# Four modulation blocks of a hybrid diffusion layer move from matmuls to dot products, and head norms and softmax rows to ScalarE

## The chip, the cores and the metric

The kernel runs on one core of one Trainium2 chip. The metric is device time in microseconds (us) of one execution: 1324.15 us is the median of three runs of the kernel before (1323.88 to 1324.64). A core has five engines that each work through a queue of their own in order: TensorE (PE in the profile, with PEld for its weight loads), VectorE (DVE), ScalarE (ACT), GpSimd (POOL) and SyncE (SP), which here only issues DMA transfers.

## What is computed

One layer of a transformer for 128 context tokens and 128 latent tokens, with width 2048. The parts that matter here:

```python
sh1, sc1, g1, sh2, sc2, g2 = silu(cond) @ w_ada + b_ada      # six modulation vectors per group
h  = rms_norm(x, norm1_w) * (1 + sc1) + sh1
qa, ka, va, qb, kb, vb, ga, gb = split(h @ w_in)             # q, k get an RMS norm per head of 128
# mixer A: window attention with a sink; mixer B: neighbourhood attention with a bias
m  = (sigmoid(ga) * (oa @ w_br_a) + sigmoid(gb) * (ob @ w_br_b)) @ w_out
x  = x + g1 * m
h2 = rms_norm(x, norm2_w) * (1 + sc2) + sh2
x  = x + g2 * (relu(h2 @ w_up) ** 2 @ w_down)
```

There are two conditions (one for the context, one for the latents), so each modulation vector exists twice. A modulation vector has 16 blocks of 128 columns. Shift and scale of one norm together are called its modulations here.

## The kernel before

All of the large products run in float32 accuracy: a weight tile of 128x1024 (a half-step, 512 KB, `raw`) is rounded by ScalarE into a high part `wH` (L101), VectorE subtracts to get the low part `wL` (L260), and TensorE adds three products, high by high, low by high, high by low. The kernel is one list of steps, `wsteps`, of 512 KB each: steps 0 to 71 are the first nine column units of `w_in` (q, k, v of both mixers), 72 to 135 the gates, then the branches, `w_out`, the up and down projections to step 455. A step holds 12 matmuls of 512 columns. Everything else is hung on a step number: `at(i, ...)` runs a piece after the matmuls of step i, and the number tables at the head of the file say which step that is. `LOOK` says how many steps ahead of TensorE the high and low parts are made, `RUN` how far ahead the transfers are put into SP's queue (`load_at`).

The nine first units are computed in chunks of the contraction (`CHUNKS` = 2, 2, 2, 4, 6 blocks of h), so that the first steps need only the first blocks of h: blocks 0 and 1 for steps 0 to 8, 2 and 3 from step 9, 4 and 5 from 18, 6 to 9 from 27, 10 to 15 from 45. Each block of h needs its block of the modulations.

A block of the modulations is made in one of two ways.

- As matmuls (`pair_load`, `pair_mm_q`, L322 and L330): four transfers of 512 KB (`araw`, shift and scale together), then 16 float32 matmuls of 256 columns, four side by side in 32-column strips of the array; the trace has 32 records for them. Two blocks share a bank, so the trace shows them as groups of 64. ScalarE copies the bank out (`ada_evac`), one step later TensorE turns it by four transposes (`ada_cols`, L348) and VectorE sums it up. `ADA_AT` has the steps for norm 1, `SS_AT` for norm 2.
- As dot products (`dot_load`, `dot`, L1398 and L1411): per block, for each of shift and scale, two transfers of 512 KB (`aT`, halves of the contraction), and for each of these two VectorE instructions of 128x1024 (one for each condition), after which a short instruction reads the accumulator. They need the conditions spread over all partitions (`cB`, L1392, two transfers of 512 KB for a half of the contraction). `DOTS1` has the steps for norm 1; `DOTS` those for the gate of the first sub-layer and norm 2 together; `DOTS2` those for the last gate.

Before, 14 blocks of norm 1 (`FB1`) and 6 of norm 2 (`FB_DVE`) are matmuls, 2 and 10 dot products; both gates are dot products altogether.

Weights' low parts can also be made without VectorE: for the steps in `LO_DMA`, ScalarE writes minus the high part (L266) and GpSimd issues a transfer that reads the weights again and adds them to it (L267).

In steps 67 to 98 the head norms run (`qk_stat`, `qk_apply`, `qk_T`, with their steps in `POST`): ScalarE squares a group's 512 columns in one instruction (L671), VectorE sums by head (L673), GpSimd takes the root, then the context half is scaled by ScalarE head by head (L683), the latent half by VectorE in one instruction (L684), and TensorE transposes. Steps 79 to 123 hold eight attention jobs (`JOBS`): scores, softmax with `exp` and sums on ScalarE, `normalise` on VectorE (L795), transposes of the probabilities (L802) which ScalarE copies out (`probT`), and the products with the values (`ps_o`, L809 and L813).

## Time and profile before

| | |
|---|---|
| median of three runs | 1324.15 us |
| the profiled execution | 1324.28 us |
| its span, first to last instruction | 1322.5 us |
| TensorE busy | 1309.0 us (99%) |
| VectorE busy | 1151.4 us (87%) |
| ScalarE busy | 890.8 us (67%) |
| moved by DMA | 419.03 MB, 317 GB/s on average |

The profiled execution lasted 1.8 us longer than its span, and 0.13 us more than the median. Busy time of an engine counts overlapping instructions once. A matmul's record lasts about 390 ns while the next one starts 227 ns later, so a stretch of TensorE is read from one start to a later one and not from the means. The same holds for VectorE and ScalarE, whose records overlap the next by some 80 to 100 ns.

### The profile page before, as it was taken

How to read it: one execution, taken by the hardware profiler on the slowest of the kernel's cores; microseconds unless marked ns; L12 is line 12 of the kernel's file. 1: busy time of each engine (PE TensorE's matmuls, PEld its weight loads, DVE VectorE, ACT ScalarE, POOL GpSimd, SP SyncE). 2: the span in 40 equal slices, each digit the busy share in tenths (PEclk: the TensorE clock that was granted, in tenths of full speed). 3: DMA queues.
4: the chain of work that ended last, by engine and by line, in shares of the span. 5: the costliest groups of instructions: out<-in, count | busy, mean ns of one | idle time of the engine just before them, and what ended most of it. 6: DMA issues, size and time to landing. Idle time of an engine off the chain costs nothing.

```text
span 1322.5 us, 18220 instructions
## 1 busy us (share of the span) xinstructions
PE 1309.0 (99%) x6388; PEld 1061.3 (80%) x6388; DVE 1151.4 (87%) x1487; ACT 890.8 (67%) x1129; POOL 87.1 (7%) x109
## 2 busy tenths in 40 slices
PE   8999999999999999999999999999999999999998
PEld 4777788788888878888888888888888888888876
DVE  4578699988898999999789889898898998979996
ACT  5634656576565545755788877968879688796772
POOL 0000000512000000000100010100101001010011
PEclk9999999999999999999999999999999999999999
DMA  9999998887689999998489998888998799899996
GB/s 375 408 408 409 406 398 344 326 286 281 200 296 343 373 377 349 323 374 306 137 289 291 290 312 273 283 300 289 292 321 281 282 341 288 295 269 366 375 334 185
DMA packets 155260, 419.03 MB, mean 317 GB/s; under 512 B 52720, under 2 KB 53984, under 8 KB 155168
## 3 DMA queue, kind: packets, MB, share of 16 engines
q1 hardware_dynamic: 146128, 386.54, 80.1%
q0 software_dynamic: 8848, 31.23, 10.3%
q8 instruction: 50, 0.82, 0.2%
q14 instruction: 42, 0.34, 0.1%
q10 hardware_dynamic: 192, 0.10, 0.0%
HBM read 390.24 MB, written 17.61 MB: 308 GB/s over the span
## 4 chain that ended last, share of the span: by engine, by line
PE 93%; DMA 3%; DVE 2%; issue 1%; POOL 0%; ACT 0%; POOLq 0%; DVEq 0%; ACTq 0%
PE acc L313 16%; PE acc L314 16%; PE acc L315 16%; PE Q L1191 6%; PE Q L1192 6%; PE Q L1193 6%; PE acc L424 5%; PE acc L425 5%; PE acc L426 5%; PE ps_ada L330 2%; DMA araw<-in_w_pair 2%; PE ps_S L756 1%; DMA wL<-in_w_down 1%; DVE aT L1411 1%; PE acc L1026 1%
## 5 line engine op out<-in xcount | busy, mean ns | idle before, releaser
L101 ACT ACTIVATE wH<-raw 128x1024 fp32r<-128x1024 f32 (+1 forms) x376 | 381.0, 1045 | 126.4 <-DMA raw<-in_w_in 17.0
L260 DVE TENSOR_TENSOR wL<-raw,wH 128x1024 fp32r<-128x1024 f32 x335 | 399.1, 1223 | 47.8 <-ACT wH L101 32.7
L424 PE MATMUL acc<-wH,hH 128*128 128x512 f32 x276 | 109.1, 395 | 0.0
L426 PE MATMUL acc<-wH,hL 128*128 128x512 f32 x276 | 107.6, 390 | 0.0
L425 PE MATMUL acc<-wL,hH 128*128 128x512 f32 x276 | 107.5, 390 | 0.0
L313 PE MATMUL acc<-wH,hH 128*128 128x512 f32 x256 | 102.6, 401 | 0.0
L315 PE MATMUL acc<-wH,hL 128*128 128x512 f32 x256 | 99.8, 390 | 0.0
L314 PE MATMUL acc<-wL,hH 128*128 128x512 f32 x256 | 99.7, 390 | 0.0
L1411 DVE CUSTOM_DVE_ANT_0 junk<-aT,cB,cols 128x1024 bf16<-128x1024 f32 x56 | 71.3, 1283 | 1.4 <-DMA cB<-silu 1.4
L1411 DVE CUSTOM_DVE_ANT_0 aT<-aT,cB,cols 128x1024 f32<-128x1024 f32 x56 | 71.6, 1288 | 0.2
L424 PEld LDWEIGHTS acc<-wH,hH 128*128 128x128 f32 x276 | 51.8, 188 | 13.6 <-issue 3.3
L1256 DVE TENSOR_TENSOR tL<-t,tH 128x1024 fp32r<-128x1024 f32 x42 | 51.2, 1220 | 11.2 <-ACT tH L101 11.2
L426 PEld LDWEIGHTS acc<-wH,hL 128*128 128x128 f32 x276 | 51.8, 188 | 11.2 <-DVE hL L105 0.2
L101 ACT ACTIVATE uH<-raw 128x1024 fp32r<-128x1024 f32 x42 | 44.4, 1058 | 23.6 <-DVE raw L1250 21.5
L425 PEld LDWEIGHTS acc<-wL,hH 128*128 128x128 f32 x276 | 51.9, 188 | 10.3
L101 ACT ACTIVATE tH<-t 128x1024 fp32r<-128x1024 f32 x42 | 44.3, 1054 | 23.5 <-DVE t L1246 18.5
L313 PEld LDWEIGHTS acc<-wH,hH 128*128 128x128 f32 x256 | 48.1, 188 | 10.5 <-issue 1.1
L314 PEld LDWEIGHTS acc<-wL,hH 128*128 128x128 f32 x256 | 48.1, 188 | 10.0 <-issue 0.7
L315 PEld LDWEIGHTS acc<-wH,hL 128*128 128x128 f32 x256 | 48.1, 188 | 10.1
L1246 DVE TENSOR_TENSOR t<-raw 128x1024 f32<-128x1024 f32 x42 | 51.2, 1218 | 1.0 <-PE acc L314 1.0
L1238 DVE TENSOR_TENSOR XL<-raw,XH 128x1024 fp32r<-128x1024 f32 x42 | 51.2, 1218 | 0.6 <-DMA sm<-dsum 0.5
L1256 DVE TENSOR_TENSOR uL<-raw,uH 128x1024 fp32r<-128x1024 f32 x42 | 51.1, 1218 | 0.0
(630 smaller groups left out, 3374.4 us busy)
## 6 DMA issues: line engine op xcount, KB each, us to landing
raw<-in_w_in SPq DMA_DIRECT2D x133, 512.0 KB, 9.0
raw<-in_w_down SPq DMA_DIRECT2D x128, 512.0 KB, 6.6
raw<-in_w_upF SPq DMA_DIRECT2D x84, 512.0 KB, 6.3
araw<-in_w_pair SPq DMA_DIRECT2D x80, 512.0 KB, 10.1
aT<-in_w_gT SPq DMA_DIRECT2D x64, 512.0 KB, 8.9
aT<-in_w_adaT SPq DMA_DIRECT2D x48, 512.0 KB, 9.9
raw<-in_w_up SPq DMA_DIRECT2D x44, 512.0 KB, 6.2
raw<-in_w_out SPq DMA_DIRECT2D x32, 512.0 KB, 10.2
```

The costliest lines, as they stand in the source:

```text
L101: act.activation(out, in_, AF.Copy)
L260: dve.tensor_tensor(st["lo"], st["raw"], st["hi"].bitcast(F32), op=OP.subtract)
L313: pe.matmul(acc[tb], sh, wh[:, k, :], start=f, stop=False, **kw)
L314: pe.matmul(acc[tb], sh, wl[:, k, :], start=False, stop=False, **kw)
L315: pe.matmul(acc[tb], sl, wh[:, k, :], start=False, stop=l, **kw)
L424: pe.matmul(acc[tb], sh, wh[:, k, :], start=kt == 0 and k == 0 and not held and not seeded, stop=False, **kw)
L425: pe.matmul(acc[tb], sh, wl[:, k, :], start=False, stop=False, **kw)
L426: pe.matmul(acc[tb], sl, wh[:, k, :], start=False, stop=last and k == 1 and not hold, **kw)
L1191: pe.matmul(acc, stat[0], hi, start=f, stop=False)
L1192: pe.matmul(acc, stat[0], lo, start=False, stop=False)
L1256: dve.tensor_tensor(b[n + "L"], v, b[n + "H"].bitcast(F32), op=OP.subtract)
L1411: dve.tensor_tensor_reduce(out, box["raw"], cB[s, tag], 1.0, dst if second else baT[:, part, fb:fb + 1], OP.mult, OP.add, dst)
```

## The change

The counts of blocks that stay matmuls fall from 14 to 12 (norm 1) and from 6 to 4 (norm 2). Three pieces of code change: the squares of the head norms are taken head by head with ScalarE's own sum, so VectorE's sum goes; the latent half is scaled by ScalarE head by head too; and each softmax row is scaled by ScalarE. The rest are other numbers in the tables: five more steps have their low parts made by the transfer (40 instead of 35), the first pair of blocks is asked for after step 3 instead of 5, the dot products of norm 1 are spread over steps 8 to 37 instead of 26 to 42, and several parts of the attention and of the up projections move by a step or a few.

```diff
-FB_DVE = 6
-FB1 = 14
+FB_DVE = 4
+FB1 = 12
-DOTS1 = [26, 26, 29, 36, 39, 40, 41, 42]
+DOTS1 = [8, 8, 9, 12, 16, 19, 24, 26, 27, 28, 31, 31, 33, 35, 37, 37]
-LO_DMA = [88, 106, 116, 131, 165, ..., 392, 410, 416, 442, 443, 449, 450]
+LO_DMA = [46, 57, 74, 92, 106, 114, 116, 127, 165, ..., 385, 410, 411, 416, 440, 442, 449]
-ADA_AT = [None, 5, 13, 16, 21, 37, 32]
+ADA_AT = [None, 3, 13, 16, 21, 35]
-SS_AT = [44, 57, 75, 75, 139, 139]
+SS_AT = [75, 75, 139, 139]
-DOTS = [32, 44, 47, 47, 49, ..., 179, 180, 183, 190]
+DOTS = [41, 44, 47, 47, 48, ..., 179, 183, 188, 190]
...
@@ qk_stat
+        ssq, r = SM(2 * nh, "ssq"), SM(2 * nh, "rq")
         for s in range(2):
-            act.activation(sq[:, s].rearrange("p h d -> p (h d)"), raw[:, s, 0:nh * HD], AF.Square)
-        ssq, r = SM(2 * nh, "ssq"), SM(2 * nh, "rq")
-        dve.tensor_reduce(ssq.rearrange("p (s h) -> p s h", s=2), sq, axis=AX.X, op=OP.add)
+            for h in range(nh):
+                act.activation(sq[:, s, h, :], raw[:, s, h * HD:(h + 1) * HD], AF.Square,
+                               accum_out=ssq[:, s * nh + h:s * nh + h + 1])
@@ qk_apply
-        for h in range(nh):
-            act.activation(x4[:, 0, h, :], x4[:, 0, h, :], AF.Copy, scale=r[:, h:h + 1])
-        dve.tensor_tensor(x4[:, 1], x4[:, 1], r[:, nh:2 * nh].unsqueeze(2).to_broadcast([P, nh, HD]), op=OP.mult)
+        for s in range(2):
+            for h in range(nh):
+                act.activation(x4[:, s, h, :], x4[:, s, h, :], AF.Copy, scale=r[:, s * nh + h:s * nh + h + 1])
@@ normalise
-            dve.tensor_tensor(prob[:, :, 0:nk], prob[:, :, 0:nk], rd.unsqueeze(2).to_broadcast([P, 4, nk]), op=OP.mult)
+            for h in range(4):
+                act.activation(prob[:, h, 0:nk], prob[:, h, 0:nk], AF.Copy, scale=rd[:, h:h + 1])
```

**The first transfers.** SP's queue just behind the half-sized first loads of steps 0 to 2, up to the third group of `araw`, which is the pair that TensorE multiplies after step 16. Before:

```order
L230 DMA raw<-in_w_in 128x1024 x6
L322 DMA araw<-in_w_pair 128x1024 x8
L230 DMA raw<-in_w_in 128x1024 x8
L322 DMA araw<-in_w_pair 128x1024 x8
L230 DMA raw<-in_w_in 128x1024 x3
L322 DMA araw<-in_w_pair 128x1024 x8
```

That third group ends with the 41st of these transfers. Now, up to the transfers ahead of the second group:

```order
L230 DMA raw<-in_w_in 128x1024 x4
L322 DMA araw<-in_w_pair 128x1024 x8
L230 DMA raw<-in_w_in 128x1024
L1394 DMA cB_384<-silu 128x1024
L1394 DMA cB_386<-silu 128x1024
L230 DMA raw<-in_w_in 128x1024 x3
L1400 DMA aT<-in_w_adaT 128x1024 x2
L230 DMA raw<-in_w_in 128x1024
L1400 DMA aT<-in_w_adaT 128x1024
L230 DMA raw<-in_w_in 128x1024 x3
L1400 DMA aT<-in_w_adaT 128x1024
L230 DMA raw<-in_w_in 128x1024 x2
```

and from there to the end of the third group:

```order
L322 DMA araw<-in_w_pair 128x1024 x8
L230 DMA raw<-in_w_in 128x1024 x2
L1400 DMA aT<-in_w_adaT 128x1024
L230 DMA raw<-in_w_in 128x1024
L322 DMA araw<-in_w_pair 128x1024 x8
```

The third group now ends with the 48th transfer: two `cB` and five `aT` have come in ahead of it. The first group ends with the 12th instead of the 14th.

**ScalarE around step 90.** ScalarE's queue from the `probT` copy of the first attention job to the two copies of the second, on which the products with the values of step 92 wait. Before:

```order
L101 ACTIVATE probT<-ps_PT 128x512
L101 ACTIVATE wH<-raw 128x1024 x2
L101 ACTIVATE T_kB_3124<-ps_qT 128x512
L715 ACTIVATE T_kB_3124<-ps_qT,cols 128x512
L683 ACTIVATE u_kB_2335<-u_kB_2335,rq 128x128 x4
L671 ACTIVATE sq<-u_qB_2179 128x512 x2
L101 ACTIVATE probT<-ps_PT 128x512 x2
```

Now:

```order
L101 ACTIVATE probT<-ps_PT 128x512
L797 ACTIVATE prob<-prob,rd 128x256 x4
L797 ACTIVATE prob<-prob,rd 128x128 x4
L101 ACTIVATE wH<-raw 128x1024 x2
L101 ACTIVATE T_kB_3116<-ps_qT 128x512
L716 ACTIVATE T_kB_3116<-ps_qT,cols 128x512
L673 ACTIVATE sq,ssq<-u_qB_2102 128x128 x8
L101 ACTIVATE probT<-ps_PT 128x512 x2
```

Two softmax scalings and six more squares stand ahead of the copies; the scaling of `u_kB` has moved behind them.

**VectorE near the end.** VectorE's queue around the low part of `a14`, one of the two inputs of the last down projections; `gc_g` are the gate's columns. Before:

```order
L1411 ISA aT,gc_g_365<-aT,cB_10942,cols 128x1024
L1411 ISA gc_g_365 128x1
L890 TENSOR_TENSOR a15L<-fTa_11433,a15H 128x1024
L260 TENSOR_TENSOR wL<-raw,wH 128x1024 x2
L1411 ISA junk,gc_g_365<-aT,cB_10940,cols 128x1024
L1411 ISA gc_g_365 128x1
L1411 ISA aT,gc_g_365<-aT,cB_10942,cols 128x1024
L1411 ISA gc_g_365 128x1
L890 TENSOR_TENSOR a14L<-fTa_11510,a14H 128x1024
L260 TENSOR_TENSOR wL<-raw,wH 128x1024 x3
```

Now:

```order
L260 TENSOR_TENSOR wL<-raw,wH 128x1024 x2
L1413 ISA aT,gc_g_365<-aT,cB_10954,cols 128x1024
L1413 ISA gc_g_365 128x1
L892 TENSOR_TENSOR a15L<-fTa_11460,a15H 128x1024
L260 TENSOR_TENSOR wL<-raw,wH 128x1024
L1413 ISA junk,gc_g_365<-aT,cB_10952,cols 128x1024
L1413 ISA gc_g_365 128x1
L260 TENSOR_TENSOR wL<-raw,wH 128x1024
L1413 ISA aT,gc_g_365<-aT,cB_10954,cols 128x1024
L1413 ISA gc_g_365 128x1
L892 TENSOR_TENSOR a14L<-fTa_11549,a14H 128x1024
L260 TENSOR_TENSOR wL<-raw,wH 128x1024 x3
```

Low parts that stood ahead of a run of dot products now stand between the last of them, and step 443, whose low part a transfer made before, is VectorE's now, while step 440 went to a transfer.

More of the change, by code (lines that the diff above doesn't have):

```diff
@@ L50 @@
 DIRECT = (3,)
-LO_DMA = [88, 106, 116, 131, 165, 180, 184, 196, 218, 224, 230, 232, 250, 251, 256, 282, 283, 288, 314, 315, 320, 329, 346, 347, 352, 378, 379, 384, 392, 410, 416, 442, 443, 449, 450]
+LO_DMA = [46, 57, 74, 92, 106, 114, 116, 127, 165, 176, 184, 196, 218, 224, 228, 232, 237, 250, 251, 256, 282, 283, 288, 314, 315, 320, 329, 346, 347, 352, 378, 379, 384, 385, 410, 411, 416, 440, 442, 449]
 LO_AHEAD = 2
-LOOK = "652322414122454322223333333122333442223323122555465644344534355765215632223444456685566655544323333333321122122312343545666445443333342344444444444434556566643344457766322234414766567565566546555331235663226676666666656665554444444444444444555555555555555544433333333344445555555555555555444444444444444455555555555555554444433244444444555555555555555546444444444444445555555555555555444444444445555555666465555555554444446656654585434443744464222433444444"
@@ L55 @@
-RUN = "411111111111121323334444433333333312222233465566655466545667777556664445555776765655445445555656776654432333333312444444555566553333333343334455555566655655555655666575565577788866677666665653476544343366555566666666666666665555555555554444566666666666666655555555555555556666666666666666555555555555555566666666555666665555577555555555666666666666666655555555555555556666666666666666555577755555575454566666676555566666666665555555776766555535444666666666"
+LOOK = "652322403022443232224443323344333232223344224755576742122334355654104521223444356685566655544323344444432222122312343544555334333333342344444433444434556566643343347544102234414766567565676546555331235663226676666666656665543233333344444444555555555566666655533333333444445555555555555555444444444444443454444455555555554444433244444444555555555555555546444444444444447555555555555555444444444445555555666465555555554444346656654565434444754464433555555555"
@@ L56 @@
+RUN = "411111111111121323334466733333333312222344576677656467645667777667663434435843654875455445555656876654432333333312444444555566577533333343334455555568877877775655666575565577788866677676665653476544343366555566666666665555565555555555554466566666666666666655555555555555556666666666666666555555555555555566666666777777776555577555555555666666666666666655555555555555556666666666666666555555556666655494566777786666676666666665755555776777555534444666666666"
 CONST_AT = [65, 69]
-ADA_AT = [None, 5, 13, 16, 21, 37, 32]
@@ L58 @@
-XS_AT = {1: 13, 2: 19, 3: 31}
-POST = {('kvA', 0): [67, 71, 76], ('qA', 0): [70, 73, 78], ('qA', 1): [72, 74, 83], ('kB', 0): [76, 86, 90], ('qB', 0): [82, 84, 93], ('kB', 1): [87, 90, 98], ('qB', 1): [90, 93, 96]}
-JOBS = [[80, 81, 81, 88, 94], [79, 83, 88, 90, 92], [87, 87, 89, 95, 100], [93, 93, 96, 102, 105], [96, 97, 100, 105, 112], [102, 103, 107, 112, 123], [105, 107, 111, 118, 123], [112, 115, 118, 121, 123]]
-SS_AT = [44, 57, 75, 75, 139, 139]
+ADA_AT = [None, 3, 13, 16, 21, 35]
+XS_AT = {1: 13, 2: 19, 3: 33}
@@ L62 @@
+POST = {('kvA', 0): [67, 71, 76], ('qA', 0): [70, 73, 78], ('qA', 1): [72, 74, 83], ('kB', 0): [76, 86, 90], ('qB', 0): [80, 84, 93], ('kB', 1): [87, 91, 99], ('qB', 1): [90, 93, 96]}
+JOBS = [[80, 81, 82, 88, 94], [79, 83, 88, 90, 92], [87, 87, 88, 95, 100], [91, 93, 96, 102, 105], [96, 97, 100, 105, 112], [102, 103, 107, 112, 123], [105, 107, 111, 118, 123], [112, 115, 118, 121, 123]]
+SS_AT = [75, 75, 139, 139]
 T_AT = [3, 4]
 PREP_IN = [5, 7]
-DOTS = [32, 44, 47, 47, 49, 50, 51, 52, 53, 56, 58, 60, 67, 67, 68, 69, 77, 78, 84, 85, 92, 93, 93, 94, 95, 99, 100, 103, 103, 104, 108, 110, 111, 111, 116, 118, 120, 120, 121, 122, 126, 126, 128, 129, 130, 132, 134, 137, 137, 138, 138, 143, 144, 145, 151, 155, 155, 158, 160, 160, 166, 167, 173, 173, 174, 175, 176, 178, 179, 180, 183, 190]
@@ L65 @@
-DOTS2 = [234, 237, 240, 266, 269, 272, 298, 301, 329, 330, 332, 363, 364, 367, 397, 398, 424, 426, 426, 428, 429, 431, 431, 432, 432, 436, 439, 439, 440, 441, 444, 444]
+DOTS = [41, 44, 47, 47, 48, 48, 50, 51, 56, 56, 57, 58, 60, 62, 63, 67, 69, 69, 70, 73, 77, 79, 84, 84, 86, 92, 93, 93, 94, 95, 98, 99, 100, 103, 103, 106, 108, 111, 111, 112, 113, 116, 116, 118, 120, 120, 121, 122, 126, 126, 128, 129, 130, 132, 134, 137, 137, 138, 138, 143, 144, 144, 151, 155, 155, 158, 160, 160, 166, 167, 173, 173, 174, 175, 176, 178, 179, 183, 188, 190]
@@ L66 @@
+DOTS2 = [234, 237, 240, 266, 269, 272, 297, 301, 329, 330, 332, 363, 364, 367, 397, 398, 424, 426, 426, 428, 431, 431, 432, 432, 433, 436, 439, 439, 440, 441, 444, 444]
 STAT_AT = [-1, 0, 8, 11]
-T_PAIR = [[6, 8], [6, 8], [8, 10], [5, 7], [10, 13], [8, 14], [12, 9]]
-P_PAIR = [[1, 3], [2, 4], [3, 4], [-1, 3], [3, 4], [3, 6], [6, 4]]
+T_PAIR = [[10, 8], [6, 8], [8, 10], [5, 7], [10, 13], [8, 14], [12, 9]]
+P_PAIR = [[1, 3], [2, 4], [3, 4], [-1, 3], [3, 4], [3, 2], [6, 5]]
 M_TE = (3,)
@@ L71 @@
 FLIP = 2
-P_UP = [2, 3]
-T_UP = [6, 11]
+P_UP = [2, 7]
+T_UP = [7, 12]
 COL = {"qA": 0, "kvA": 1024, "qB": 1536, "kB": 2560, "vB": 3584, "gA": 4608, "gB": 6656}
```

## The prediction

> **What bounds the kernel now.** I read the page's busy rows and its chain first, then the waits of TensorE, then windows by stage.

> ```profile
> span 1322.5 us, 18220 instructions
> PE 1309.0 (99%) x6388; PEld 1061.3 (80%) x6388; DVE 1151.4 (87%) x1487; ACT 890.8 (67%) x1129; POOL 87.1 (7%) x109
> ...
> PE 93%; DMA 3%; DVE 2%; issue 1%; POOL 0%; ACT 0%; POOLq 0%; DVEq 0%; ACTq 0%
> ```

> TensorE is busy for 99% of the span and 93% of the chain that ended last, so the kernel is as long as TensorE's work and the few waits inside it. TensorE's waits, those that the change comes near:

> ```profile
> PE acc L314 <- DMA wL<-in_w_down: 1.7, 1, 1.7
> PE ps_ada L330 <- DMA araw<-in_w_pair: 1.3, 2, 0.7
> ...
> PE acc L315 <- DVE a14L L890: 1.1, 1, 1.1
> ```

> So little waiting can be won; what can be won is work. But a busy share of 99% doesn't say that the other engines have room. Busy us by stretch:

> ```profile
> core 0: us, PE busy (x) PEld busy (x) DVE busy (x) ACT busy (x) POOL busy (x), PEclk, DMA share, GB/s
> 0.00:50.00 50.00, 45.21 (x297) 25.96 (x298) 23.36 (x45) 29.10 (x49) 3.11 (x12) 1.00 0.99 386
> 50.00:155.00 105.00, 105.00 (x709) 80.39 (x708) 75.25 (x110) 50.45 (x71) 0.00 (x0) 1.00 1.03 408
> 228.00:330.00 102.00, 102.00 (x544) 83.61 (x543) 90.73 (x131) 67.97 (x136) 32.91 (x29) 1.00 0.83 301
> 300.00:350.00 50.00, 50.00 (x257) 41.21 (x255) 42.56 (x65) 32.10 (x72) 6.83 (x6) 1.00 0.72 259
> ```

> Until 155 us the DMA share is at its full value, with 408 GB/s (512 KB in 1.28 us), while VectorE has 30 us free. In the attention (228 to 330) the transfers have room, and VectorE is the full one: 11 us free. So the change pays in a different coin in each stage: transfers early, VectorE and ScalarE in the attention.

> **The change: TensorE.** The chain shows what a group of two matmul blocks costs:

> ```profile
> 72.39 0.44 PE ps_sel L348 x4
> 78.31 3.59 PE ps_ada L330 x64
> ...
> 171.70 1.86 PE ps_ada L330 x32
> ...
> 209.15 1.86 PE ps_ada L330 x32
> ```

> Norm 1 loses one group of two blocks, 3.59 + 0.44 = 4.03 us. Norm 2 loses its two blocks that stand alone after steps 44 and 57, 2 x 1.86 and one group of transposes, 4.16 us. Together **−8.19 us**, all of it on the path.

> **The change: VectorE.** Two rows one behind the other give start-to-start times; the groups give the rest.

> ```profile
> 1248.19 1.28 DVE L1411 CUSTOM_DVE_ANT_0 junk<-aT,cB,gc_g 128x1024 bf16<-128x1024 f32 x1
> 1249.40 4.63 DVE L260 TENSOR_TENSOR wL<-raw,wH 128x1024 fp32r<-128x1024 f32 x4
> 1253.94 1.28 DVE L1411 CUSTOM_DVE_ANT_0 aT<-aT,cB,gc_g 128x1024 f32<-128x1024 f32 x1
> L673 DVE TENSOR_REDUCE ssq<-sq 128x8 f32<-128x1024 f32 x6 | 7.3, 1217 | 2.2 <-ACT sq L671 2.2
> L684 DVE TENSOR_TENSOR u_qB<-u_qB,rq 128x512 f32<-128x512 f32 x2 | 1.4, 685 | 0.0
> L795 DVE TENSOR_TENSOR prob<-prob,rd 128x1024 f32<-128x1024 f32 x4 | 4.9, 1224 | 0.1
> L795 DVE TENSOR_TENSOR prob<-prob,rd 128x512 f32<-128x512 f32 x4 | 2.8, 692 | 0.1
> ```

> A dot product takes 1.21 us (1248.19 to 1249.40), a low part 4.54/4 = 1.135. Four blocks are 4 x 2 (shift, scale) x 2 halves x 2 conditions = 32 dot products: +38.7. By size, on the low part's rate, 1024 columns cost about 1.13, 512 about 0.6 and 256 about 0.33. Away go seven head sums (6 x 1.13 + 0.6 = 7.4), seven scalings (6 x 0.6 + 0.33 = 3.9), eight softmax scalings (4 x 1.14 + 4 x 0.61 = 7.0), five low parts (5.7), and the two `ada_cols` sums (about 0.8). Net **about +14 us** on an engine with 171 us free in all. Hidden, if it falls where there is room; the two stretches below decide that.

> **The change: ScalarE.** Its queue around the first two attention jobs:

> ```profile
> 286.10 0.37 ACT L781 ACTIVATE prob<-ps_S,nm 128x128 f32<-128x128 f32 x1
> 286.46 0.36 ACT L781 ACTIVATE prob<-ps_S,nm 128x128 f32<-128x128 f32 x1
> 291.38 1.14 ACT L671 ACTIVATE sq<-u_qB 128x512 f32<-128x512 f32 x2
> 292.42 0.67 ACT L715 ACTIVATE T_qA<-ps_qT,cols 128x512 f32<-128x512 f32 x1
> 297.10 1.28 ACT L683 ACTIVATE u_qB<-u_qB,rq 128x128 f32<-128x128 f32 x4
> 298.28 1.06 ACT L101 ACTIVATE wH<-raw 128x1024 fp32r<-128x1024 f32 x1
> 315.08 1.27 ACT L683 ACTIVATE u_kB<-u_kB,rq 128x128 f32<-128x128 f32 x4
> 316.40 1.15 ACT L671 ACTIVATE sq<-u_qB 128x512 f32<-128x512 f32 x2
> 317.46 1.06 ACT L101 ACTIVATE probT<-ps_PT 128x512 f32<-128x512 f32 x2
> ```

> A 128-column scaling costs (298.28 − 297.10)/4 = 0.295, a 512-column square (292.42 − 291.38)/2 = 0.52, a 128-column `exp` with its sum 0.36. A square of one head with its sum was not run; between the scaling and 0.43 (`exp` and half a step more) I take 0.385, near the `exp`, which also reads an accumulator. Squares go from 14 to 52: 20.0 − 6.9 = +13.1. Scalings: 26 x 0.295 = +7.7. Softmax rows: 16 of 128 columns and 16 of 256 (0.40, between 0.295 and the square's 0.52): +11.1. Five more negated high parts: about +4.8. One group's copies less: −1.0. Net **about +36 us**, of which some 25 fall into 228 to 330, where ScalarE then has 93 of 102. No time of its own on the path, but the queue in order gets tight.

> [...]

> **Where it meets the path, 1: the first transfers.** TensorE can't multiply a pair before its last transfer has landed. Before:

> ```profile
> 32.38 10.16 DMA araw<-in_w_pair
> 42.58 0.64 PE ps_ada L330 x8
> 74.55 9.27 SPq L322 DMA_DIRECT2D araw<-in_w_pair  x8
> 81.84 0.50 PE L424 MATMUL acc<-wH,hH 128*128 128x512 f32 x1
> ```

> A transfer lands about 10.16 us after its issue; in the saturated stretch one more lands every 1.28 us. The third group starts at 78.31 and step 17 at 81.84. By the queues in the section on the change this group ends with transfer 41 before and 48 after. The fourth group before stands at 47 to 54 (issued from 74.55 on, one per about 1.2 to 1.3), so place 48 is issued at 74.55 + 1.28 = 75.8 and lands at 86.0. What is left for TensorE then is the last few matmuls (0.64 for 8 in the row at 42.58), so step 17 starts at about 86.65, not 81.84: **+4.8 us**. As a check, seven places at 1.28 are 9.0, against a slack of about 4 that the earlier first group (place 12, not 14) and the wait inside the pair use up. An earlier stall of some 3 us at the first group, which now stands after step 3 where TensorE is there sooner than its transfer, is contained in it, not added. Bounds: 0 (if step 16's loads were late already in both) to 9.0.

> **2: VectorE in steps 8 to 41.** A dot product waits for its `aT`, and behind it in VectorE's queue stand the low parts of the steps, for which TensorE waits. To 75.25 of 105 come 16 dot products (19.4) and some 4 us that moved, less 2.4: about 97 of 110, the stretch being longer by term 1. Where a dot product waits for a transfer of the saturated queue, the low parts have LOOK's mostly 2 to 4 steps of 2.7 us (12 matmuls) as cover, though 0 at steps 7 and 9 of the changed table. Between 0 and +9 (rival C) I take **+0.5**, near nothing.

> **3: the attention.** Job 2's `probT` copies are done at 318.5, and the products start when they have what they need:

> ```profile
> 319.31 1.72 PE ps_o L809 x4
> ```

> 0.8 us to spare. Ahead of the copies 8 squares of 0.385 (3.1) stand in place of 1.04, the scaling of `u_kB` (1.3) has moved behind, and two softmax scalings (2.8) stand earlier, in ScalarE's wait of that stretch. 3.1 − 1.04 − 1.3 = 0.8, so the cover is just used; one more slipped `wH` costs up to 1. The new wait (ScalarE's scaling on VectorE's reciprocal) has `wH` of the next steps behind it, a look-ahead of 2 or 3 steps covers that. Between 0 and +3 I take **+0.7**.

> **4: the end.** The wait of 1.7 us is for a low part by transfer in the down projection:

> ```profile
> 1272.37 9.64 DMA wL<-in_w_down
> 1282.05 0.50 PE acc L314
> ```

> It is that of step 443, which is VectorE's now: −1.7, with up to 0.2 late next at step 437's. The 1.1 for `a14L` stays, since a low part more stands ahead of it and two less behind: **−1.5** (−2.8 to +1.5).

> The other moves (steps of gates, of norm 2's dot products, up projections): their bytes are equal (a group's 8 `araw` become 8 `aT`), and VectorE has room for them after 330; counted as nothing, up to +1 if a low part by transfer (46, 57, 74 are new, 1.28 us each, POOL issues them) lands late.

> **The sum** against the profiled execution's 1324.28 (0.13 above the median of 1324.15; 1.78 lies outside the span): 1324.28 − 8.19 + 4.8 + 0.5 + 0.7 − 1.5 = **1320.6 us**.

> **The rivals.**
> B. Full gain: early on, place 48 costs TensorE nothing, since stalls of the saturated stretch are taken back where the queue drains. For it: DMA share falls to 0.72 later. Against: a stall of TensorE isn't taken back by an engine that is busy for 99%. 1324.28 − 8.19 − 1.5 = 1314.6.
> D. The change doesn't do what it says: the work leaves TensorE, and its waits take all of it. Term 1 as forecast, attention +3 and the end's wait stays at another step: 1324.28 − 8.19 + 4.8 + 0.5 + 3 = 1324.4.
> C. Slower: VectorE in steps 8 to 41 becomes the bound. Before it idles 30 us there; the added 21 fit if no more than about 11 of the idle are forced (waits for `raw` and `aT` in a queue in order). If 20 are forced, TensorE waits 9 more: 1320.6 + 9 = 1329.6. For it: dot products of step 8 on need transfers just issued; against: TensorE waited for no low part there before.

> **How the numbers follow.** 0.2% (2.65 us) is about what a measurement of this kernel can tell from no change. Forecast 0.50 (its own range 1317.5 to 1323.5; 0.40 of it faster, 0.10 same), B 0.18 (faster), D 0.18 (same), C 0.14 (slower). So faster 0.58, same 0.28, slower 0.14. The range leaves out C and the lower edge of B: 1314 to 1326.

> **What would show it.** In the profile after, step 17's first matmul at 86 to 87 and a wait of `ps_ada` of some 5 us in all on `araw` (term 1); no wait of `acc` on a `wL` of L260 before 160 us (2, against C); `ps_o` on `probT` under 1 us (3); no wait on `wL<-in_w_down` above 0.3 (4); 128 records of `L330` less. Step 17 at 82, or waits for low parts of 9 us early, would make it wrong.

## The result, and the profile after

The changed kernel takes 1330.41 us (median of five runs, 1329.53 to 1331.6); beside it on the same chip the kernel before took 1323.88. The ratio is 1.0049, 95% interval 1.0038 to 1.0059: slower by half a per cent, where 1320.6 us was forecast. The profile is of an execution with a span of 1328.5 us, 6.0 more than before.

The page of the changed kernel, the rows that answer to those of before:

```profile
span 1328.5 us, 18153 instructions
...
PE 1304.6 (98%) x6251; PEld 1058.3 (80%) x6252; DVE 1163.4 (88%) x1515; ACT 919.2 (69%) x1279; POOL 92.8 (7%) x114
...
PE 85%; DMA 9%; DVE 4%; ACT 1%; issue 1%; POOL 0%; SPq 0%; ACTq 0%; DVEq 0%
```

VectorE has 12 us more and ScalarE 28 (forecast +14 and +36). TensorE's share of the chain fell from 93% to 85%, and the transfers' rose from 3% to 9%: TensorE waits more, it stands still for 23.9 us of the span (1328.5 − 1304.6) instead of 13.5. Its waits in the changed kernel (us in total, times, longest):

```profile
PE acc L314 <- DMA wL<-in_w_in: 5.6, 1, 5.6
PE ps_ada L330 <- DMA araw<-in_w_pair: 4.2, 7, 0.7
...
PE ps_sel L348 <- ACT S L101: 1.3, 3, 0.6
...
PE ps_S L757 <- DVE rd L795: 0.7, 1, 0.7
PE acc L314 <- DVE wL L260: 0.7, 2, 0.5
PE acc L313 <- ACT acc L101: 0.6, 1, 0.6
...
PE acc L315 <- DVE a14L L892: 0.6, 1, 0.6
```

One wait stands out, 5.6 us in one piece, and it is for a `wL` that a transfer makes (L266 and L267), not for VectorE. To see what it is worth, I took the start of each step's first matmul from TensorE's rows of both kernels and subtracted:

| start of step | before, us | after, us | after − before | since the row above |
|---|---|---|---|---|
| 16 | 75.43 | 79.44 | +4.0 | +4.0 |
| 17 | 81.84 | 86.74 | +4.9 | +0.9 |
| 23 | 102.95 | 108.71 | +5.8 | +0.9 |
| 59 | 214.15 | 211.07 | −3.1 | −8.8 |
| 63 | 225.17 | 222.77 | −2.4 | +0.7 |
| 75 | 257.81 | 263.51 | +5.7 | **+8.1** |
| 103 | 358.39 | 365.16 | +6.8 | +1.1 |
| 146 | 492.81 | 499.24 | +6.4 | −0.3 |
| the end (span) | 1322.5 | 1328.5 | +6.0 | −0.4 |

Of the 4.9 us at step 17, 4.0 are lost by step 8 already (49.23 before, 53.24 now), most of them at the first group of matmul blocks: TensorE has five waits for its transfers there, 2.9 us in all, where it had one of 0.6. A wait of 0.4 for a copy of ScalarE follows at step 8, and the third group adds one wait for its transfers. One of the five, and that one:

```profile
36.31 0.64 PE L330 MATMUL ps_ada<-araw,early 128*32 128x256 f32 x8 [0.64 <-DMA araw<-in_w_pair]
...
86.17 0.64 PE L330 MATMUL ps_ada<-araw,early 128*32 128x256 f32 x8 [0.64 <-DMA araw<-in_w_pair]
```

At step 63 the change is 2.4 us ahead. Step 74 alone costs 8.1. TensorE's rows of the changed kernel there (start, duration, and in brackets the wait before):

```profile
252.69 0.39 PE L313 MATMUL acc<-wH,hH 128*128 128x512 f32 x1
258.65 0.80 PE L314 MATMUL acc<-wL,hH 128*128 128x512 f32 x1 [5.58 <-DMA wL<-in_w_in]
259.25 0.63 PE L315 MATMUL acc<-wH,hL 128*128 128x512 f32 x1
...
263.51 0.51 PE L313 MATMUL acc<-wH,hH 128*128 128x512 f32 x1
263.86 0.40 PE L314 MATMUL acc<-wL,hH 128*128 128x512 f32 x1
```

The wait is 5.58 us. From 259.25 to 263.51 ten matmuls start 0.426 us apart instead of 0.227; with the two at either end that is 12 slow ones, and 8.1 − 5.6 = 2.5 us. The granted clock is 0.93 in 250 to 300, where it was 1.00 before. Why the transfer was late stands in GpSimd's rows, beside the one of ScalarE that negates the high part:

```profile
237.90 1.06 ACT L266 ACTIVATE wL<-wH 128x1024 fp32r<-128x1024 f32 x1
```

```profile
234.43 1.26 POOL L652 TENSOR_SCALAR_AFFINE_SELECT bias<-bias 64x384 f32<-64x384 f32 x1 [45.85 <-DMA bias<-in_rpb_qk]
...
244.65 1.42 POOL L654 TENSOR_SCALAR_AFFINE_SELECT bias<-bias 64x384 f32<-64x384 f32 x1
246.16 1.07 POOL L147 TENSOR_SCALAR rs<-ssq 128x4 f32<-128x4 f32 x1
247.32 1.94 POOL L148 TENSOR_TENSOR rq<-rs,pw 128x4 f32<-128x4 f32 x1
249.23 0.94 POOL L267 DMA_DIRECT2D wL<-in_w_in  x1
```

ScalarE is done at 238.96. The transfer is issued at 249.23, 10.3 us later, because GpSimd, which issues it, first makes the eight masks of the attention's bias and a root. It lands 9.4 us after that. The same masks stand in the rows of the kernel before, at the same time, with no transfer behind them:

```profile
235.64 0.68 POOL L652 TENSOR_SCALAR_AFFINE_SELECT bias<-bias 64x384 f32<-64x384 f32 x1 [223.29 <-DMA bias<-in_rpb_qk]
...
247.09 1.87 POOL L148 TENSOR_TENSOR rq<-rs,pw 128x4 f32<-128x4 f32 x1
248.91 0.63 POOL L719 DMA_DIRECT2D out_new_b_v<-u_vB  x1
```

GpSimd is busy for 7% of the span, and these 13 us are the stretch in which the new transfer is due. The 10.3 us between ScalarE's end and the issue agree with a transfer that stands in GpSimd's queue, behind the masks and the root (234.43 to 249.23).

### The profile page after: what moved, and what is told of

It reads as the page before. It is cut to its first block, busy times and chain, and to the rows that moved or that the text cites. A ratio compares the mean times of both kernels' runs of the same rounds, so it can differ in the third digit from the quotient of the medians.

```text
span 1328.5 us, 18153 instructions
## 1 busy us (share of the span) xinstructions
PE 1304.6 (98%) x6251; PEld 1058.3 (80%) x6252; DVE 1163.4 (88%) x1515; ACT 919.2 (69%) x1279; POOL 92.8 (7%) x114
## 4 chain that ended last, share of the span: by engine, by line
PE 85%; DMA 9%; DVE 4%; ACT 1%; issue 1%; POOL 0%; SPq 0%; ACTq 0%; DVEq 0%
PE acc L314 16%; PE acc L313 16%; PE acc L315 16%; PE Q L1194 6%; PE Q L1195 6%; PE Q L1193 6%; PE acc L424 3%; DMA araw<-in_w_pair 3%; PE acc L425 3%; PE acc L426 3%; DMA raw<-in_w_in 2%; DMA aT<-in_w_gT 1%; DMA raw<-in_w_down 1%; PE ps_ada L330 1%; DVE junk L1413 1%; DVE aT L1413 1%
## 5 line engine op out<-in xcount | busy, mean ns | idle before, releaser
L101 ACT ACTIVATE wH<-raw 128x1024 fp32r<-128x1024 f32 (+1 forms) x376 | 380.7, 1045 | 132.2 <-DMA raw<-in_w_in 45.8
L260 DVE TENSOR_TENSOR wL<-raw,wH 128x1024 fp32r<-128x1024 f32 x330 | 393.5, 1225 | 50.5 <-ACT wH L101 31.6
L424 PE MATMUL acc<-wH,hH 128*128 128x512 f32 x276 | 108.7, 394 | 0.4 <-ACT u_kB L101 0.4
L314 PE MATMUL acc<-wL,hH 128*128 128x512 f32 x256 | 101.0, 395 | 5.6 <-DMA wL<-in_w_in 5.6
L315 PE MATMUL acc<-wH,hL 128*128 128x512 f32 x256 | 101.0, 394 | 0.0
L1413 DVE CUSTOM_DVE_ANT_0 aT<-aT,cB,cols 128x1024 f32<-128x1024 f32 x64 | 81.6, 1287 | 0.2
L1413 DVE CUSTOM_DVE_ANT_0 junk<-aT,cB,cols 128x1024 bf16<-128x1024 f32 x64 | 81.7, 1290 | 0.0
L424 PEld LDWEIGHTS acc<-wH,hH 128*128 128x128 f32 x276 | 51.8, 188 | 13.3 <-issue 1.6
L314 PEld LDWEIGHTS acc<-wL,hH 128*128 128x128 f32 x256 | 48.8, 191 | 16.2 <-DMA wL<-in_w_in 6.0
L101 ACT ACTIVATE uH<-raw 128x1024 fp32r<-128x1024 f32 x42 | 44.4, 1058 | 24.9 <-DVE raw L1252 22.7
L101 ACT ACTIVATE tH<-t 128x1024 fp32r<-128x1024 f32 x42 | 44.3, 1055 | 23.4 <-DVE t L1248 18.7
L315 PEld LDWEIGHTS acc<-wH,hL 128*128 128x128 f32 x256 | 48.7, 190 | 10.3
```

The source lines that it names most:

```text
L101: act.activation(out, in_, AF.Copy)
L260: dve.tensor_tensor(st["lo"], st["raw"], st["hi"].bitcast(F32), op=OP.subtract)
L314: pe.matmul(acc[tb], sh, wl[:, k, :], start=False, stop=False, **kw)
L315: pe.matmul(acc[tb], sl, wh[:, k, :], start=False, stop=l, **kw)
L424: pe.matmul(acc[tb], sh, wh[:, k, :], start=kt == 0 and k == 0 and not held and not seeded, stop=False, **kw)
L1413: dve.tensor_tensor_reduce(out, box["raw"], cB[s, tag], 1.0, dst if second else baT[:, part, fb:fb + 1], OP.mult, OP.add, dst)
```

## The experiments

Theory Q: the transfer of step 74 stood in GpSimd's queue; its wait and the slow matmuls behind it are the 8.1 us. Rivals: V, VectorE and the transfers are short there and the wait only shows it; T, the transfer takes too long whenever it is issued. All kernels were timed beside the kernel before on the same chip; times are medians, and "kernel 1" below is that of run 1, "kernel 3" that of run 3, and so on.

**1. Step 74 back to VectorE (no74).**

```diff
-LO_DMA = [46, 57, 74, 92, ...]
+LO_DMA = [46, 57, 92, ...]
```

> The changed kernel with one number taken out: the low part of step 74 is VectorE's again. Theory Q (the transfer that adds the weights to the negated high part stood 10.3 us in GpSimd's queue behind the eight masks of the attention's bias, TensorE waited 5.6 us for it and then ran 12 matmuls at about 0.43 instead of 0.23 us, 2.4 us more): about 1330.4 - 8.0 = 1322.4 us, step 75 starting at about 255.4 instead of 263.5. Rival V (VectorE and the transfers are the bound there, the transfer only shows it): another wait of some us takes its place, 1327 to 1331 us.

Measured: 1324.17 us, ratio 1.0008 (0.9999 to 1.0016). One number of the table carries the whole slowdown: 6.2 us go. The other 1.8 of the 8.0 came back in a wait that the stall had covered. VectorE's low part for step 75 now stands behind a run of six dot products; TensorE's wait in this run:

```profile
PE acc L314 <- DVE wL L260: 2.0, 2, 1.5
```

V has a part of its own then, a small one. The profiled execution is the slowest of the eleven (1326.63 us): at step 8 it has a wait of 2.2 us for a copy of ScalarE, where the changed kernel has 0.4, and slow matmuls behind it.

**2. Masks earlier (bias62)**, and **3. masks later (bias74)**: in both the transfer of step 74 is kept, and the bias is asked for after another step, so that GpSimd makes the masks ahead of the transfer's time, or behind it.

```diff
-CONST_AT = [65, 69]
+CONST_AT = [65, 62]     # bias62
+CONST_AT = [65, 74]     # bias74
```

> The changed kernel, step 74's low part still by transfer, but the bias that the masks work on is asked for seven steps earlier, so that GpSimd makes the masks before the transfer is due. Theory Q: the transfer is issued about 0.3 us after ScalarE's negation (239), lands near 249, TensorE at 252.7 doesn't wait: 1322 to 1323 us. Rival T (the transfer takes too long under the load of the other transfers, whenever it is issued after the negation): the wait stays at 3 us or more, 1327 us or more.

> The changed kernel, step 74's low part by transfer, with the bias asked for five steps later, so that the masks stand behind that transfer in GpSimd's queue (and nothing else of VectorE's constants moves). Theory Q: issued at about 239.3, landed by 249, no wait at step 74: 1322 to 1323 us, if the first job that needs the masks is later than they are. Rival T (the transfer takes too long whenever it is issued): 1327 us or more.

Measured: 1326.16 us, ratio 1.0022 (1.0012 to 1.0032), and 1324.27 us, ratio 1.0004 (0.9995 to 1.0013). GpSimd's rows with the masks later:

```profile
235.53 2.06 POOL L148 TENSOR_TENSOR rq<-rs,pw 128x4 f32<-128x4 f32 x1
238.52 0.93 POOL L267 DMA_DIRECT2D wL<-in_w_in  x1 [0.92 <-ACT wL L266]
...
247.24 1.64 POOL L652 TENSOR_SCALAR_AFFINE_SELECT bias<-bias 64x384 f32<-64x384 f32 x1 [0.86 <-DMA bias<-in_rpb_qk]
```

The transfer now waits for ScalarE and for nothing else, and the wait of step 74 is gone in both kernels, with the transfer kept: T falls, Q stands. But the late issue cost more than its place in the queue: issued at 238.52 the transfer landed 5.4 us later, issued at 249.23 in the changed kernel 9.4. The stretches from issue to landing with the masks later, then in the changed kernel (the last two numbers are the DMA share and GB/s):

```profile
238.50:244.00 5.50, 5.50 (x26) 4.56 (x25) 5.50 (x7) 4.91 (x20) 1.93 (x4) 1.00 0.69 150
...
249.20:258.60 9.40, 3.88 (x18) 2.87 (x16) 9.01 (x19) 8.81 (x32) 9.09 (x10) 0.91 1.03 325
```

The DMA engines were full in the later stretch and not in the earlier one (shares of 1.03 and 0.69). It is the same in runs 2, 4 and 5: 5.8, 10.6 and 10.0 us at shares of 0.69, 1.02 and 1.03. That the load made the landing slower is likely but was not tried by itself. Both times are above what I expected. With the masks earlier, the bias's transfer goes ahead of VectorE's small constants, and a low part behind these comes late at step 62; with the masks later, steps 75 and 76 show what the stall had covered, 0.5 us for a low part and 0.5 for a group's last transfer:

```profile
PE acc L425 <- DVE wL L260: 2.7, 1, 2.7
```

```profile
256.39 0.50 PE L314 MATMUL acc<-wL,hH 128*128 128x512 f32 x1 [0.50 <-DVE wL L260]
...
262.85 0.64 PE L330 MATMUL ps_ada<-araw,early 128*32 128x256 f32 x8 [0.51 <-DMA araw<-in_w_pair]
```

The first of these two fences is of the masks earlier (TensorE's waits), the second of the masks later (its rows).

**4. The kernel before with 74 in the table (before74).**

```diff
-LO_DMA = [88, 106, ...]
+LO_DMA = [74, 88, 106, ...]
```

> The kernel before, with 74 added to the steps whose low part is a transfer, and nothing else. Theory Q: its masks run to 245.9 and a root to 248.9, so the transfer is issued at about 248.9, lands at about 258.3, and TensorE, which needs it at about 255.3, waits some 3 us, with the slow matmuls behind it up to 5.4: 1326.9 to 1329.3 us. Rival V (it takes the rest of the change, with its fuller ScalarE and transfers, to make the transfer late): 1323 to 1325 us.

Measured: 1327.82 us, ratio 1.0039 (1.0026 to 1.0052); in its profile:

```profile
PE acc L314 <- DMA wL<-in_w_in: 3.1, 1, 3.1
```

The number costs time in a kernel without any of the other edits too: no more transfers, no fuller ScalarE is needed. It costs less than 8.1 there, since TensorE comes to step 74 later (255.09 against 252.69) and so waits 3.1 instead of 5.6. Its step 75 starts 4.5 us later than before: 3.1 of wait, and 1.4 from seven slow matmuls that begin 1.6 us behind it.

**5. Two masks less (mask6)**: the second row's upper corners of the attention's bias are left unmasked.

```diff
                 v = bias[q, :, r2, NA_COLS:]
+                if r == 1:
+                    continue
```

> The changed kernel with two of the eight masks of the bias left out (so two corners of the attention's bias are not masked). Theory Q: the transfer is issued 2.9 us earlier and TensorE waits 2.7 instead of 5.6 us. If the slow matmuls behind the wait come with any wait of some us, 1330.4 - 2.9 = 1327.5 us; if they come only with a long one, 1330.4 - 2.9 - 2.4 = 1325.1 us. Rivals V and T: no change, 1330 us.

Measured: 1326.19 us, but spread from 1323.04 to 1329.7 in twelve runs, where the changed kernel's five lay within 2.1. The profiled run, one of the longest with 1329.04 us, has a wait of 3.2 us and 13 slow matmuls behind it, so they don't need a wait of 5.6. The wait shrank nearly as Q says (to 2.7). The median stands between the two numbers that I expected, and what differs from run to run isn't seen in one profile.

**6. The first group later (pair5)**, on kernel 1, and **7. with the dot products later as well (early_both).**

```diff
-ADA_AT = [None, 3, 13, 16, 21, 35]
+ADA_AT = [None, 5, 13, 16, 21, 35]                        # pair5, early_both
-DOTS1 = [8, 8, 9, 12, 16, 19, 24, 26, ...]
+DOTS1 = [19, 20, 21, 22, 23, 24, 24, 26, ...]             # early_both
```

> The changed kernel without 74 (1324.2 us by itself) and with the first group of matmul blocks after step 5 again instead of 3. By the prediction's first term the stall at the first group is contained in that of the third: its last transfer keeps place 48, step 17 still starts at about 86.7 and the time stays at 1324 us (within 0.7). Rival: the stall at the first group is the price, and the time falls by up to 4 us, to 1320.

> As the run with the first group after step 5, and the first six dot products of norm 1 moved behind step 18, so that the third group ends with transfer 43 instead of 48. If the place is what sets TensorE's start, step 17 starts at about 82 to 82.5 instead of 86.7 and the gain is kept: 1319.7 us. Rival: the transfers are due by step 45 whatever their order, the 408 GB/s give the gain back in another wait before 190 us: 1323 to 1325 us.

Measured: 1323.98 us, ratio 1.0002 (0.9993 to 1.0011), and 1331.65 us, ratio 1.0061 (1.0049 to 1.0074). With the first group later, step 17 starts at 86.9, as in the changed kernel. That was meant to show that the stall at the first group is contained in the third's, but it doesn't: TensorE waits for the first group here as well (four waits between 41.5 and 45.4, 2.6 us in all), and step 16 starts at 80.20, even later than the changed kernel's 79.44. With the dot products out of the way as well, the first group has landed at 42.23 (before 42.54), the third at 79.62, TensorE has one wait of 0.6 us for the two, and step 17 starts at 81.4. So the order of the early transfers does set it; but from step 22 on low parts and sums come late, and step 30 starts 13 us later than before. Waits of this kernel:

```profile
PE acc L425 <- DVE wL L260: 4.2, 2, 2.4
...
PE acc L424 <- DVE u_kvA L437: 2.2, 1, 2.2
PE acc L314 <- DVE wL L260: 2.2, 3, 1.5
```

Between 82 and 136 us TensorE waits 5.7 us for VectorE, which is busy for 48.9 of these 54 us, 2.0 for transfers of the fourth group and 1.9 for a copy of ScalarE. So the larger part of the price comes from VectorE, a smaller one from the transfers that my rival named: 16 dot products from step 19 on stand too close together.

**8. A few dot products later (dots_b)**, on kernel 3.

```diff
-DOTS1 = [8, 8, 9, 12, 16, 19, 24, ...]
+DOTS1 = [8, 9, 17, 18, 19, 20, 24, ...]
```

> The changed kernel with its masks behind the transfer of step 74, and the dot products of norm 1 at 8, 9, 17, 18, 19, 20 instead of 8, 8, 9, 12, 16, 19 (the other ten unchanged), so that the third group ends with transfer 46 instead of 48. If a few dot products fit into VectorE behind step 17: step 17 at about 84.2 and 1321.7 us. Rival: VectorE has no room there; waits for low parts between steps 17 and 30 take the 2.6 us back and more: 1324.3 us or above.

Measured: 1327.22 us, ratio 1.0027 (1.0017 to 1.0036). The same in small: TensorE waits 2.9 us for VectorE's sums (`u_vB`, L437) around step 22. Step 17 starts at 85.91, not at 84.2. The third group, with transfer 46, has landed at 83.43 and TensorE doesn't wait for it; it comes 4.1 us late, as it has been since step 8. So the third group's place alone is worth 0.8 us, and an earlier one gains nothing more while the first group stalls. Neither table tried here has both, early transfers for the groups and room on VectorE.

**9. Head norms on VectorE again (heads_dve)**, on kernel 1: the code of `qk_stat` and `qk_apply` of before.

```diff
-        for s in range(2):
-            for h in range(nh):
-                act.activation(sq[:, s, h, :], raw[:, s, h * HD:(h + 1) * HD], AF.Square, accum_out=...)
+            act.activation(sq[:, s].rearrange("p h d -> p (h d)"), raw[:, s, 0:nh * HD], AF.Square)
+        dve.tensor_reduce(ssq.rearrange("p (s h) -> p s h", s=2), sq, axis=AX.X, op=OP.add)
...
+        dve.tensor_tensor(x4[:, 1], x4[:, 1], r[:, nh:2 * nh].unsqueeze(2).to_broadcast([P, nh, HD]), op=OP.mult)
```

> The changed kernel without 74, with the head norms' squares and scalings as before (VectorE sums by head and scales the latent half; about 11 us more for VectorE, 21 less for ScalarE). If ScalarE's queue is what costs in the attention (the prediction's +0.7): about 1323.5 us. Rival: VectorE's time is what is short from step 60 to 100, where low parts wait behind dot products: 1327 us or more.

Measured: 1329.6 us, ratio 1.0042 (1.0029 to 1.0056): 5.4 slower than kernel 1. The rival was right: VectorE is what is short there.

```profile
PE acc L314 <- DVE wL L260: 5.0, 3, 4.3
```

**10. Softmax rows on VectorE again (softmax74)**, on kernel 3.

```diff
-            for h in range(4):
-                act.activation(prob[:, h, 0:nk], prob[:, h, 0:nk], AF.Copy, scale=rd[:, h:h + 1])
+            dve.tensor_tensor(prob[:, :, 0:nk], prob[:, :, 0:nk], rd.unsqueeze(2).to_broadcast([P, 4, nk]), op=OP.mult)
```

> The changed kernel with its masks behind the transfer of step 74, and the softmax rows scaled by VectorE as before (7.0 us more for VectorE, 11 less for ScalarE). If the wait of 0.7 us for a reciprocal behind which ScalarE scales is the price of that edit: 1323.4 us. Rival: VectorE is what is short in steps 79 to 123, the low parts behind the eight scalings come late: 1326 us or more.

Measured: 1323.1 us, ratio 0.9999 (0.999 to 1.0008), near the 1323.4 expected: in steps 79 to 123 VectorE has room, and the wait for the reciprocal falls from 0.7 to 0.2 us. It is the lowest time found, but its interval overlaps that of kernel 3 (0.9995 to 1.0013), and it is no different from the kernel before.

**11. Norm 2's part alone (norm2_only)**, on kernel 3, with norm 1 as before.

```diff
-FB1 = 12
+FB1 = 14
-DOTS1 = [8, 8, 9, 12, ...]
+DOTS1 = [26, 26, 29, 36, 39, 40, 41, 42]
-ADA_AT = [None, 3, 13, 16, 21, 35]
+ADA_AT = [None, 5, 13, 16, 21, 37, 32]
```

(and `XS_AT` and the first 60 entries of `LOOK` and `RUN` of before)

> The changed kernel with its masks behind the transfer of step 74 (1324.3 us by itself), and with norm 1 as before: 14 matmul blocks, its dot products, groups and the look-aheads of the first 60 steps from the kernel before. Norm 2's two blocks stay dot products, the ScalarE edits and the rest stay. If norm 1's two blocks give TensorE 4.0 us and cost it 4.9 (step 17) and 0.8 (step 23), leaving them costs 1.7 us: about 1322.5 us. Rival: VectorE, freed of 16 dot products, also takes the waits of steps 63 and 75 away: 1321 or less; or the old early tables don't fit the rest: above 1325.

Measured: 1325.95 us, ratio 1.0018 (1.0008 to 1.0028), a miss: the old early tables don't fit the rest. TensorE is level with before until step 44, gains the block of step 44, and loses 1.9 us at once at step 45 to a low part of VectorE and 3.2 at steps 75 and 76. How much norm 2's part is worth with tables made for it stays open.

**12. The small constants earlier (best62)**, on kernel 10.

```diff
-CONST_AT = [65, 74]
+CONST_AT = [62, 74]
```

> The run with the softmax rows on VectorE and the masks behind the transfer (1323.1 us), with the small constants (rotary tables, head weights, caches) asked for three steps earlier, since VectorE waits for them with the low part of step 62 behind it (2.1 us idle, TensorE 1.3 us). If that wait is all: 1322.0 to 1322.5 us, below the kernel before by 0.1%. Rival: the three weight loads that the constants pass come later by as much, a wait at steps 59 to 62 in its place: 1323 to 1325 us.

Measured: 1330.53 us, ratio 1.005 (1.0036 to 1.0063), the same mistake once more, on another queue. VectorE's instruction on the constants now stands in its queue ahead of the low part that step 59 needs, and waits for its transfer. VectorE's rows, then TensorE's wait:

```profile
213.47 0.36 DVE L620 TENSOR_SCALAR early<-early 128x384 f32<-128x384 f32 x1 [10.20 <-DMA early<-in_k_norm_b]
...
214.89 2.35 DVE L260 TENSOR_TENSOR wL<-raw,wH 128x1024 fp32r<-128x1024 f32 x2
```

```profile
PE acc L425 <- DVE wL L260: 4.8, 1, 4.8
```

Twelve slow matmuls follow it, and step 60 starts 7.2 us later against step 59 than before. My rival named the three weight loads; it was the waiting constant itself.

## Why the prediction was wrong

By its own steps:

- **TensorE's work, −8.19.** Right: −8.8 between steps 23 and 59 (the group of two blocks of norm 1, the two single ones of norm 2, their transposes, and the changes between shapes around them: before, a group starts 0.32 us behind the last 512-column matmul, at 77.93 and 78.25, and the second matmul behind it 0.33 us after the first, at 81.84 and 82.17, where matmuls of a step start 0.227 apart; about 0.2 for each of three groups, as an estimate).
- **1, the first transfers, +4.8.** Right in size, and right that place 48 bounds step 17: it landed at 86.13 (forecast 86.0), step 17 started at 86.74 (86.65). But the stall at the first group, which I counted as contained, had with the 0.4 behind it cost 4.0 of the 4.9 us before that, and without the third group's wait step 17 still comes 4.1 us late (kernel 8). Two bounds lie 0.8 us apart here, and the sum named the later one. That place 48 alone, without the first stall, would give the 86.7 as well follows from its landing and was not run. The changed kernel's row:

```profile
86.74 0.50 PE L424 MATMUL acc<-wH,hH 128*128 128x512 f32 x1
```

- **2, VectorE in steps 8 to 41, +0.5.** Near: +0.9 at step 23 (a copy of ScalarE behind a late load) and +0.7 before step 63. Rival C did not happen, though its 1329.6 lies close to the time: TensorE waited for no low part of L260 before 160 us. But VectorE had less room than I reckoned, 101.78 of 110 against 97, and kernels 7 and 8 show the edge.

```profile
50.00:160.00 110.00, 108.33 (x672) 83.47 (x671) 101.78 (x155) 55.81 (x78) 0.00 (x0) 1.00 1.03 408
```

- **"The other moves … counted as nothing, up to +1 if a low part by transfer (46, 57, 74 are new, 1.28 us each, POOL issues them) lands late."** This is the step that failed: step 74 cost 8.1. I priced the transfer's bytes and named who issues it, but didn't look at what GpSimd does at that time. The masks stood in the trace of before, from 235.64 to 248.96, and a sum was to be had from it: issued at 248.9, landed some 9.6 us later by my own row of term 4, so at 258.5, for a low part that TensorE wanted at 255.3 before and earlier after the gain. Steps 46 and 57, with nothing ahead of them on GpSimd, had 3.5 and 12.7 us to spare.
- **3, the attention, +0.7.** +1.1 from step 75 to 103. A square of one head costs 0.295 (242.68 to 242.97 and on), not 0.385, and ScalarE got 28 us more, not 36; 0.7 of the price was a wait that I hadn't named: I had looked at `wH` behind ScalarE's wait for the reciprocal, and it was TensorE's scores that waited. Scalings of 128 and 256 columns start 0.293 and 0.400 us apart in the changed kernel (four from 299.73 to 300.90; 315.67 to 316.07 and on), near the 0.295 and 0.40 reckoned.

```profile
242.68 0.29 ACT L673 ACTIVATE sq<-u_qA 128x128 f32<-128x128 f32 x1
...
242.97 0.29 ACT L673 ACTIVATE sq<-u_qA 128x128 f32<-128x128 f32 x1
```

- **4, the end, −1.5.** −0.4. The wait for the transfer of step 443 went and a shorter one for `a14L` stayed, but three new ones (ScalarE's copy, two low parts) took most of it: 0.6, 0.5 and 0.2.

Without step 74's 8.1 the terms would add up to 1324.28 + 6.0 − 8.1 = 1322.2 us by the profiles; kernels 1 and 3 give 1324.2, for the most part since waits that the stall had covered appear: from step 75 to step 76 kernel 3 takes 7.9 us, 1.5 longer than before. So even with the mistake mended the change brings nothing that can be measured: the 8.8 us that TensorE saved are spent on the early groups' transfers (4.9), on VectorE's and ScalarE's queues (0.9, 0.7, 1.1) and on steps 75 and 76 (1.5). Rival D's 1324.4 lies close to that, but by other terms: it had 3 for the attention and nothing for steps 63 and 75.

## What to carry to other kernels

The transfer of step 74 stood 10.3 us in the queue of the engine that issues it: before moving work to an engine that is busy for 7%, read its rows in the very stretch in which the work is due, and add what stands ahead of it. In kernel 12 a VectorE instruction that waited 10.20 us for its transfer delayed the low part behind it, and TensorE waited 4.8 us: moving a load earlier can be as dear as moving it later. When a stall goes, look for the waits that it covered before counting it as gain.

## What the runs showed of the hardware

```profile
259.90:263.20 3.30, 3.30 (x10) 2.52 (x9) 0.42 (x1) 0.62 (x1) 0.16 (x1) 0.50 1.03 419
```

```profile
38.60:45.30 6.70, 6.37 (x26) 3.81 (x27) 0.00 (x0) 2.54 (x5) 0.00 (x0) 0.50 1.02 405
```

Behind single waits of 5.6, 4.3, 3.1 and 2.2 us (the changed kernel, heads_dve, before74, and no74 at step 8) ten, seven, seven and five matmuls have a record of 0.63 us instead of 0.39; behind one of 2.2 us in early_both (119.79) none has. In the kernel before, whose longest wait is 1.7 us, the clock is 1.00 from 0 to 1320. But no bound can be read from this, since the stretch of kernel 10 lies at the first group, and none of that kernel's waits for `araw` is longer than 0.7 us (3.7 in all, in seven). In the changed kernel, with five waits of 0.3 to 0.6 us at the first group (2.9 in all), the clock is 1.00 from 0 to 250, and in kernel 3, with 4.8 us of waits for `araw` in nine, it is 1.00 over the span. It costs little at that place: step 17 starts at 86.95 in kernel 10, which has the slow stretch, and at 87.14 in kernel 3, which hasn't. The first slow matmul of kernel 4 begins 1.6 us after the wait (258.56 to 260.21):

```profile
258.56 0.50 PE L314 MATMUL acc<-wL,hH 128*128 128x512 f32 x1 [3.08 <-DMA wL<-in_w_in]
...
260.21 0.63 PE L314 MATMUL acc<-wL,hH 128*128 128x512 f32 x1
260.63 0.63 PE L315 MATMUL acc<-wH,hL 128*128 128x512 f32 x1
```

So the price of the late transfer was not its wait alone: 5.6 us of wait and 2.5 of slow matmuls in the changed kernel, 3.1 and 1.4 in kernel 4. What sets the clock down these runs don't show.

**VectorE's and GpSimd's instructions took longer side by side.** While the masks run in the changed kernel (234.43 to 246.07), a dot product takes up to 1.56 us, where one takes 1.28 ahead of them and behind them, and a low part 1.55 (244.10), where one at 228.17 takes 1.22. VectorE's rows:

```profile
245.58 1.56 DVE L1413 CUSTOM_DVE_ANT_0 junk<-aT,cB,cols 128x1024 bf16<-128x1024 f32 x1
...
247.07 1.28 DVE L1413 CUSTOM_DVE_ANT_0 junk<-aT,cB,cols 128x1024 bf16<-128x1024 f32 x1
```

The masks of the changed kernel take 1.26 to 1.53 us, with VectorE busy on such instructions. In run 2, with the masks earlier, one takes 0.55 while VectorE stands still:

```profile
217.49 0.55 POOL L652 TENSOR_SCALAR_AFFINE_SELECT bias<-bias 64x384 f32<-64x384 f32 x1
```

So the transfer of step 74 stood behind 11.6 us of masks (234.43 to 246.07) while VectorE was busy with such instructions; at the pace of two in run 2 (217.49 to 218.61) eight would take about 4.5 us, as an estimate. Whether one engine slows the other, and why, was not tried.
